# A hybrid decoder step on one core: the weight-quarter sums of every second channel tile of the up-projection, made early and kept in DRAM

## The chip, the core and the metric

The kernel runs on one core of a Trainium2 chip. The metric is device time in microseconds: the median of several runs of the whole program. The core's engines work side by side and wait for each other through semaphores: TensorE (PE in the rows) for matrix products, VectorE (DVE), ScalarE (ACT) and GpSimd (POOL) for elementwise work, and queues on SyncE (SP) and GpSimd that start transfers between DRAM and on-chip memory.

## The reference

One inference step of one decoder layer, for a prompt of 2064 tokens (16 of them learned) and 8 samples of one token. All is float32. Cut to the trunk and the part that the change touches:

```
def conv_ffn(h, hist, w_up, conv_w, conv_b, w_down):
    L = h.shape[1]
    up = h @ w_up                       # 1024 -> 2 x 2816
    g, v = up[..., :D_FF], up[..., D_FF:]
    ext = jnp.concatenate([hist.astype(g.dtype), g], axis=1)
    c = conv_b + conv_w[0] * ext[:, 0:L]
    for k in range(1, CONV_W):
        c = c + conv_w[k] * ext[:, k:k + L]
    out = (jax.nn.gelu(c) * v) @ w_down
    return out, ext[:, -(CONV_W - 1):]

def trunk(x, ...):
        h = rmsnorm(x, norm1_g[l])
        proj = h @ w_in[l]              # u_pool | u_ssm | gate_pool | gate_ssm
        y_pool, hp = pool_mixer(u_pool, ...)
        y_s, hr, hi = ssm_mixer(u_ssm, ...)
        y_ssm = glu_out(y_s, w_glu[l])
        x = x + (gate_pool * y_pool + gate_ssm * y_ssm) @ w_out[l]
        h2 = rmsnorm(x, norm2_g[l])
        f, hc = conv_ffn(h2, st_conv[l], w_up[l], conv_w[l], conv_b[l], w_down[l])
        x = x + f
        y = rmsnorm(x, norm_f_g)
```

## The kernel before

Every float32 product is made of three matmuls on values split into a rounded high and a low part (`split`: ACT casts the high part, L125; DVE or GpSimd subtracts it for the low part, L126; `mm3`: the matmuls of L144 to L146).

The program runs in stages. First the tokens are normalized piece by piece (`norm_piece`: DVE multiplies by the norm and the weight g1B at L258, PE transposes at L194), and the first part's input projections (sixteen calls of `u_ssm` and `u_pool`) and gates (`gate_ssm` eight times, `gate_pool` four times) are made, to about 224 us. Then come the setup of the state-space model (its tile mul is filled by GpSimd from L546 on), the model itself with the second part's gates (to about 690 us), the merge, the output projection and second norm (to about 1110 us), the up-projection with convolution (to about 2012 us), and the down-projection.

The up-projection is a 2x2 block product by seven products in place of eight (Winograd's form of Strassen's scheme). A call of `up(s, f, ...)` here is named a turn: s is one of three parts of the tokens, f one of 22 tiles of 128 channels, and a turn has 7 products of 12 matmuls of 128x344, 84 in all. The weights of a turn are four quarters of 128 partitions x 4 x 128: a11 and a12 of the gate columns' rows (wr1), a21 and a22 of the value columns' (wr2). The scheme needs four sums of them, s3 = a11 - a21, s1 = a21 + a22, s2 = s1 - a11 and s4 = a12 - s2. `w_ops(s, f)` makes them on GpSimd for s = 0 (L1129 to L1132), and SP stores them in DRAM (`WS`, 256 and 768 KB); for s = 1 and 2 it loads them from there instead of a21, with a11, a12 and a22. The weights are made two tiles ahead of their turn.

Products leave PSUM through ACT's copies (m and u, L1177) and DVE's additions into g (L1185, L1187). In part 0 ACT then copies the samples' columns (gsamp, L1195), GpSimd makes v (L1189) and moves two columns of g (L1196), and ACT and DVE make the convolution c (L1207 to L1216). The seventh product of a turn, and what follows it, is done by `up_end` inside the next turn: DVE multiplies one half of c by the product, GpSimd the other by v (L1224). For odd f, `up_end` (so in the turn of the next even f) also makes the combinations e that the down-projection needs, on DVE (L1244 to L1247), and GpSimd stores c and e in DRAM (`SD`, L1239).

The order on each engine is fixed when the program is built: a scheduler places instructions by priority and by their place in the code. Within an engine's row nothing overtakes.

Of the kernel before, what the change touches and what calls it, by code (L numbers as in the profile page):

```python
# [9 lines left out]
F32 = mybir.dt.float32  # L10
# [5 lines left out]
MUL, ADD, SUB, MAX = ALU.mult, ALU.add, ALU.subtract, ALU.max  # L16
# [3 lines left out]
P = 128  # L20
D = 1024
KT = 8
DFF = 2816
NF = 22
# [18 lines left out]
NU = 2 * NH * NSB  # L43
NT = 1024
WIN = (2, 4, 8, 16)


def _bits(x, n):
# [14 lines left out]
def hybrid_kernel(ctx, tc, x_prompt, x_sample, state_pool, state_re, state_im, state_conv, meta,  # L63
# [4 lines left out]
    V, S, T, GP = nc.vector, nc.scalar, nc.tensor, nc.gpsimd  # L68
    dma, gdma = nc.sync.dma_start, nc.gpsimd.dma_start
# [3 lines left out]
    w_in, w_glu, w_out, w_up, w_down = w_in[0], w_glu[0], w_out[0], w_up[0], w_down[0]  # L73
    pool_w = pool_w[0]

    def pool(name, bufs=1, space=None, side=None):
        kw = dict(name=name, bufs=bufs)
        if space is not None:
            kw["space"] = space
        if side is not None:  # L80
            kw["side"] = side
        if space is not DRAM:
            kw["reuse_waits"] = "tile"
        return tc.tile_pool(**kw)
# [7 lines left out]
    def bank(tag, name):  # L92
        return psum.tile([P, 512], F32, tag=tag, name=name, bufs=4)
# [12 lines left out]
    WS = dram.tile([NF, P, 4, 4, P], F32, name="WS")  # L106
# [96 lines left out]
    h1pool = gsc.enter_context(pool("h1pool"))  # L203
    evac = gsc.enter_context(pool("evac"))
    h0ctx = ExitStack()
    h0pool = h0ctx.enter_context(pool("h0pool"))
    hT = []
    for j, (a, b) in enumerate(PIECES):
# [11 lines left out]
    def norm_piece(j):  # L220
        a, b = PIECES[j]
        tiles = []
        off = 0
        if j == 0:
            tiles.append((0, 24, None))
            off = 24
        while off < b - a:
            tiles.append((off, P, a + off - 24))
            off += P
        ss = xpool.tile([P, 4], F32, tag="ss", name=f"ss_{j}", bufs=2)  # L230
        rs = xpool.tile([P, 4], F32, tag="rs", name=f"rs_{j}", bufs=2)
        if j == 0:
            V.memset(ss[:, 0:1], 1.0)
            tiles = [tiles[1], tiles[0], tiles[2]]
        xs = []
        for i, (o, m, p0) in enumerate(tiles):
            i = (1, 0, 2)[i] if j == 0 else i
            xt = xpool.tile([P, D], F32, tag="xt", name=f"xt_{j}_{i}", bufs=4)
            if p0 is None:
                dma(xt[0:14, :], meta[0:14, :])  # L240
                dma(xt[14:22, :], x_sample)
                dma(xt[22:24, :], meta[14:16, :])
            else:
                dma(xt, x_prompt[p0:p0 + P, :])
            xs.append((i, xt))
        for (o, m, p0), (i, xt) in zip(tiles, xs):
            junk = xpool.tile([P, D], BF16, tag="junk", name=f"junk_{j}_{i}", bufs=1)
            S.activation(junk[0:m], xt[0:m], AF.Square, accum_out=ss[0:m, i:i + 1])
            if j == 0:
                rsqrt(xpool, rs[:, i:i + 1], ss[:, i:i + 1], 1, f"n1_{j}_{i}")  # L250
        if j == 0:
            dma(g1B, norm1_g[0].partition_broadcast(P))
        else:
            rsqrt(xpool, rs[:, 0:len(tiles)], ss[:, 0:len(tiles)], len(tiles), f"n1_{j}")
        for (o, m, p0), (i, xt) in zip(tiles, xs):
            for q in range(2):
                c = slice(512 * q, 512 * (q + 1))
                V.scalar_tensor_tensor(xt[0:m, c], xt[0:m, c], rs[0:m, i:i + 1], g1B[0:m, c], op0=MUL, op1=MUL)  # L258
            transpose_split(xt, m, hT[j][0], hT[j][1], o, f"n1_{j}_{i}")
# [9 lines left out]
    def w_in_tile(m, name, eng=None):  # L269
        return load_w([(0, KT, w_in[:, m * P:(m + 1) * P].rearrange("(k p) c -> p k c", p=P))], name, eng)  # L270
# [25 lines left out]
    def u_pool(m, j, w):  # L296
# [17 lines left out]
        else:  # L314
            S.copy(up[:, 0:n], ps[:, 0:n])
            dma(rows[:, 16 + a - 8:16 + b - 8], up[:, 0:n])
            if j == 5:
# [3 lines left out]
                if m == 3:  # L321
                    dma(pool_p[0, 0], psamp[0:15, :])

    norm_piece(0)
    u_cols = (4, 5, 6, 7, 0, 1, 2, 3)
    u_w = [w_in_tile(m, f"u0_{m}", GP) for m in u_cols[:2]]
    norm_piece(1)
    for n, (i, j) in enumerate([(0, 0), (1, 0), (0, 1), (1, 1)] + [(i, j) for i in range(2, 8) for j in PARTS[0]]):
        m = u_cols[i]
        if i == len(u_w):  # L330
            u_w.append(w_in_tile(m, f"u0_{m}"))
        (u_ssm if m >= 4 else u_pool)(m % 4, j, u_w[i])
        if n in (1, 5, 9, 13):
            norm_piece(2 + n // 4)
    with tc.issue_after(w_ins[0]):

        vrow = xpool.tile([P, P], F32, tag="sr", name="vrow", bufs=2)
        for r0, n, ap in ((0, 8, norm1_g), (8, 8, norm2_g), (16, 8, pool_scale), (24, NF, conv_b), (46, 3 * NF, conv_w)):
            src = ap.rearrange("o (k p) -> (o k) p", p=P) if ap is not conv_w else ap[0].rearrange("w (k p) -> (w k) p", p=P)
            dma(vrow[r0:r0 + n, 0:P], src)  # L340
        pt = bank("B", "pt_c")
        T.transpose(pt[:, 0:112], vrow[0:112, 0:P], ident[0:112, 0:112])
        V.tensor_copy(colv, pt[:, 0:112])
        dma(pool_s[0, :, 0:14, :].rearrange("b r c -> b (r c)"),
            state_pool[:, 1:15, :].rearrange("b r c -> b (r c)"))
        dma(conv_s[0, :, 0, :], state_conv[:, 1, :])

        sv = state_conv.rearrange("b k (f p) -> (b k f) p", p=P)
        stv = stT.rearrange("p b k f -> p (b k f)")
        for r0 in range(0, 352, P):  # L350
            n = min(P, 352 - r0)
            sr = xpool.tile([P, P], F32, tag="sr", name=f"sr_{r0}", bufs=2)
            dma(sr[0:n], sv[r0:r0 + n])
            pq = bank("B", f"psc_{r0}")
            T.transpose(pq[:, 0:n], sr[0:n], ident[0:n, 0:n])
            V.tensor_copy(stv[:, r0:r0 + n], pq[:, 0:n])

        st = xpool.tile([120, 512], F32, name="st")
        dma(st, state_pool.rearrange("b r c -> (b r) c"))
        for g, w in enumerate(WIN):  # L360
            pq = bank("B", f"pst_{g}")
            T.transpose(pq[:, 0:120], st[:, g * P:(g + 1) * P], ident[0:120, 0:120])
            V.tensor_reduce(ssum[:, g, :], pq[:, 0:120].rearrange("p (b r) -> p b r", b=NS)[:, :, 16 - w:15],
                            axis=mybir.AxisListType.X, op=ADD)
# [7 lines left out]
    def pool_d(g, j):  # L372

        a, b = PIECES[j]
        w = WIN[g]
        pos0 = a - 8 if j else 14
# [66 lines left out]
    for m in range(8):  # L443
        for _ in gate_ssm(m, 0):
            pass
    for g in range(4):
        for _ in gate_pool(g, 0):
            pass
    h0ctx.close()


# [361 lines left out]
    for c in range(2):  # L813
        rows = slice(c * P, (c + 1) * P)
# [289 lines left out]
    def w_ops(s, f):  # L1104


        r1 = upA.tile([P, KT, P], F32, tag="r", name=f"wr1_{s}_{f}", bufs=4)
        r2 = upA.tile([P, KT, P], F32, tag="r", name=f"wr2_{s}_{f}", bufs=4)
        st = upA.tile([P, 3, 4, P], F32, tag="st", name=f"ws_{s}_{f}", bufs=2)
        later(r1, w_up[:, f * P:(f + 1) * P].rearrange("(k p) c -> p k c", p=P))  # L1110
        value = w_up[:, DFF + f * P:DFF + (f + 1) * P].rearrange("(k p) c -> p k c", p=P)
        ops = {}

        def sp(key, src):
            if (s, f) == (0, 0) and key in ORDER[:3]:
                hi, lo = [fw0.tile([P, 4, P], F32R, name=f"w{n}0_{key}") for n in "hl"]
            else:
                made[0] += 1
                pl, n = (fw, 6) if made[0] % 9 < 6 else (fw2, 3)
                hi = pl.tile([P, 4, P], F32R, tag="wh", name=f"wh{key}_{s}_{f}", bufs=n)  # L1120
                lo = pl.tile([P, 4, P], F32R, tag="wl", name=f"wl{key}_{s}_{f}", bufs=n)
            split(src, hi, lo)
            ops[key] = (hi, lo)

        a11, a12, a21, a22 = r1[:, 0:4, :], r1[:, 4:8, :], r2[:, 0:4, :], r2[:, 4:8, :]
        s1, (s2, s3, s4) = a21, [st[:, i] for i in range(3)]
        if s == 0:
            later(r2, value)
            GP.tensor_tensor(s3, a11, a21, op=SUB)  # L1129
            GP.tensor_tensor(s1, a21, a22, op=ADD)  # L1130
            GP.tensor_tensor(s2, s1, a11, op=SUB)
            GP.tensor_tensor(s4, a12, s2, op=SUB)  # L1132
            later(WS[f, :, 0], s1)
            later(WS[f, :, 1:4], st)
        else:
            later(s1, WS[f, :, 0])
            later(st, WS[f, :, 1:4])
            later(a22, value[:, 4:8])
        srcs = {1: a11, 6: s2, 7: s3, 5: s1, 3: s4, 4: a22, 2: a12}

        def make(key):
            if key not in ops:
                sp(key, srcs[key])
            return ops[key]

        return make
# [434 lines left out]
```

## Time and profile before

| | |
|---|---|
| runs | 2485.01, 2492.08, 2494.64 us; median 2492.08 us |
| profiled execution | 2488.14 us, span 2486.4 us from first to last instruction |
| mean granted clock of PE | 0.985 of full speed |
| busy over the span | PE 2387.1 us (96%), DVE 1688.9 (68%), ACT 980.3 (39%), GpSimd 942.2 (38%) |
| moved by DMA | 429.25 MB, 173 GB/s |

Busy time of PE is matmuls only; its weight loads run beside them. The granted clock is the speed that the chip's throttle allowed PE, relative to full speed. Idle time of an engine costs something only where another engine, in the end PE, waits for what it should have made. The rows shown below come from the page of the profiled execution and from views of its trace.

### The profile page before, as it was taken

What the parts mean: (1) busy time and instruction counts of PE and PEld (TensorE: products, weight loads), DVE (VectorE), ACT (ScalarE), POOL (GpSimd) and SP (SyncE); (2) the same over time, 40 slices, a digit from 0 to 9 for tenths busy, and PEclk for the clock granted to TensorE, in tenths of its full rate; (3) what the DMA queues carried; (4) which work ended last, traced back from release to release, by engine and by line L of the source; (5) the groups of instructions that cost most, each with busy time, mean ns of one, the idle gap of its engine ahead of it and who ended that gap; (6) DMA issues with size and microseconds to landing.
All of it is one profiled execution on the core that took longest, in us unless ns stands there. A gap on an engine that the chain in (4) does not pass through costs nothing. (4 is left out here: it accounts for less than half of the span.)

```text
span 2486.4 us, 37900 instructions
## 1 busy us (share of the span) xinstructions
PE 2387.1 (96%) x13628; PEld 2225.6 (90%) x13628; DVE 1688.9 (68%) x2916; ACT 980.3 (39%) x1814; POOL 942.2 (38%) x1189
## 2 busy tenths in 40 slices
PE   7999999999999999978899999999999999999997
PEld 6999999999999978878889999999999987878876
DVE  7635779987384244479888987678777764555766
ACT  5422222222342122254444555556555543332432
POOL 1000287985023220147666543233333223331383
PEclk9999999999999999999999999999999999999999
DMA  7544533333477666565555665555655578645673
GB/s 197 169 126 114 103 111 109 111 111 110 103 210 221 174 206 180 170 187 168 177 173 173 209 205 193 180 173 173 211 185 189 178 223 274 215 149 170 210 247 120
DMA packets 431375, 429.25 MB, mean 173 GB/s; under 512 B 89612, under 2 KB 353160, under 8 KB 431171
## 3 DMA queue, kind: packets, MB, share of 16 engines
q1 hardware_dynamic: 394723, 356.77, 47.9%
q0 software_dynamic: 11120, 40.40, 4.7%
q10 hardware_dynamic: 25344, 29.66, 3.4%
q8 instruction: 107, 1.75, 0.3%
q14 instruction: 81, 0.66, 0.1%
HBM read 297.20 MB, written 129.86 MB: 172 GB/s over the span
## 5 line engine op out<-in xcount | busy, mean ns | idle before, releaser
L144 PE MATMUL puX<-x,wh 128*128 128x344 f32 x1056 | 344.0, 329 | 31.3 <-ACT u L1177 16.7
L145 PE MATMUL puX<-x,wh 128*128 128x344 f32 x1056 | 344.4, 326 | 1.1 <-DVE x L126 1.1
L146 PE MATMUL puX<-x,wl 128*128 128x344 f32 x1056 | 340.3, 325 | 0.0
L1499 PE MATMUL pd<-th,sh 128*128 128x512 f32 x600 | 236.2, 396 | 3.6 <-ACT sh L125 2.7
L1501 PE MATMUL pd<-th,sl 128*128 128x512 f32 x600 | 236.5, 396 | 3.1 <-DVE sl L126 3.1
L1500 PE MATMUL pd<-tl,sh 128*128 128x512 f32 x600 | 238.3, 397 | 0.6 <-DVE tl L126 0.6
L126 DVE TENSOR_TENSOR wl<-wr,wh 128x512 fp32r<-128x512 f32 x264 | 214.0, 814 | 32.2 <-ACT wh L125 31.5
L144 PEld LDWEIGHTS puX<-x,wh 128*128 128x128 f32 x1056 | 202.9, 193 | 36.3 <-ACT u L1177 19.9
L125 ACT CAST wh<-wr 128x512 fp32r<-128x512 f32 x264 | 163.0, 619 | 162.3 <-PE puX L145 93.0
L126 DVE TENSOR_TENSOR sl<-sr,sh 128x512 fp32r<-128x512 f32 x154 | 134.7, 908 | 116.7 <-ACT sh L125 113.6
L145 PEld LDWEIGHTS puX<-x,wh 128*128 128x128 f32 x1056 | 203.5, 193 | 1.5 <-DVE x L126 1.4
L1274 POOL TENSOR_TENSOR tr<-tr,tr 128x512 f32<-128x512 f32 x77 | 111.1, 1444 | 244.2 <-DMA tr<-in_w_down_dram 235.7
L146 PEld LDWEIGHTS puX<-x,wl 128*128 128x128 f32 x1056 | 203.1, 193 | 0.0
L126 DVE TENSOR_TENSOR wl<-ws,wh 128x512 fp32r<-128x512 f32 x198 | 169.9, 864 | 43.7 <-ACT wh L125 43.5
L144 PE MATMUL puZ<-x,wh 128*128 128x344 f32 x528 | 169.9, 322 | 2.7 <-DVE g L1185 2.7
L146 PE MATMUL puZ<-x,wl 128*128 128x344 f32 x528 | 168.8, 320 | 2.0 <-DVE wl L126 2.0
L145 PE MATMUL puZ<-x,wh 128*128 128x344 f32 x528 | 169.5, 321 | 0.0
L125 ACT CAST wh<-ws 128x512 fp32r<-128x512 f32 x198 | 122.0, 619 | 103.3 <-PE puX L145 73.4
L125 ACT CAST sh<-sr 128x512 fp32r<-128x512 f32 x154 | 88.3, 618 | 177.5 <-PE pd L1500 154.5
L1499 PEld LDWEIGHTS pd<-th,sh 128*128 128x128 f32 x600 | 114.1, 190 | 31.9 <-ACT sh L125 3.2
L1501 PEld LDWEIGHTS pd<-th,sl 128*128 128x128 f32 x600 | 113.9, 190 | 29.3 <-DVE sl L126 4.2
L1500 PEld LDWEIGHTS pd<-tl,sh 128*128 128x128 f32 x600 | 114.1, 190 | 25.9 <-DVE tl L126 1.0
(532 smaller groups left out, 6696.2 us busy)
## 6 DMA issues: line engine op xcount, KB each, us to landing
wr<-in_w_up_dram SPq DMA_DIRECT2D x88, 512.0 KB
tr<-in_w_down_dram SPq DMA_DIRECT2D x150, 256.0 KB
sr<-SD SPq DMA_DIRECT2D x70, 512.0 KB
ws<-WS SPq DMA_DIRECT2D x44, 768.0 KB
WS<-ws SPq DMA_DIRECT2D x22, 768.0 KB
SD<-c POOLq DMA_DIRECT2D x44, 344.0 KB, 3.5
SD<-e POOLq DMA_DIRECT2D x22, 516.0 KB, 7.3
wr<-WS SPq DMA_DIRECT2D x44, 256.0 KB
```

The source lines that it names most:

```text
L125: S.copy(hi, raw)
L126: return (eng or V).tensor_tensor(lo, raw, hi.bitcast(F32), op=SUB)
L144: T.matmul(ps, wh, xh, start=start, stop=False, **kw)
L145: T.matmul(ps, wh, xl, start=False, stop=False, **kw)
L146: T.matmul(ps, wl, xh, start=False, stop=stop, **kw)
L1274: GP.tensor_tensor(raws[0], raws[0], raws[n + 1], op=op)
L1499: T.matmul(acc[j], xh[:, c], th, start=k == 0, stop=False)
L1500: T.matmul(acc[j], xh[:, c], tl, start=False, stop=False)
L1501: T.matmul(acc[j], xl[:, c], th, start=False, stop=k == NP - 1)
```

## The change

For even f, a generator `pre_sums` makes the four sums at the beginning of the program, in two units for each f (each with half of the rows): four loads of 128x2x128 from w_up and one store into WS, all from GpSimd's queue, and four GpSimd operations of 128x256 between them. A unit's tile is in a pool of two buffers. The code calls for a unit after each of the last ten of the sixteen projections, after each `gate_ssm` and after each `gate_pool`: 22 units. In `w_ops`, part 0 of an even f then loads as parts 1 and 2 do; part 0 of an odd f is as before. Lines of the up-projection stand 24 further down than before (L1129 is L1153, L1196 is L1220, L1224 is L1248).

```
+PRE = range(0, NF, 2)
...
     h0ctx = ExitStack()
+    pre = h0ctx.enter_context(pool("pre"))
...
+    def pre_sums():
+
+        for f in PRE:
+            for h in range(2):
+                t = pre.tile([P, 4, 2, P], F32, tag="pre", name=f"pre_{f}_{h}", bufs=2)
+                a22, a11, a21, a12 = [t[:, i] for i in range(4)]
+                for a, k, c in ((a22, 4, DFF), (a11, 0, 0), (a21, 0, DFF), (a12, 4, 0)):
+                    rows, cols = (k + 2 * h) * P, c + f * P
+                    gdma(a, w_up[rows:rows + 2 * P, cols:cols + P].rearrange("(k p) c -> p k c", p=P))
+                GP.tensor_tensor(a22, a21, a22, op=ADD)
+                GP.tensor_tensor(a21, a11, a21, op=SUB)
+                GP.tensor_tensor(a11, a22, a11, op=SUB)
+                GP.tensor_tensor(a12, a12, a11, op=SUB)
+                gdma(WS[f, :, :, 2 * h:2 * h + 2, :], t)
+                yield
+
+    pre_units = pre_sums()
...
         if n in (1, 5, 9, 13):
             norm_piece(2 + n // 4)
+        if n >= 6:
+            next(pre_units)
...
     for m in range(8):
         for _ in gate_ssm(m, 0):
             pass
+        next(pre_units)
     for g in range(4):
         for _ in gate_pool(g, 0):
             pass
+        next(pre_units)
     h0ctx.close()
...
-        if s == 0:
+        if s == 0 and f not in PRE:
             later(r2, value)
             GP.tensor_tensor(s3, a11, a21, op=SUB)
             GP.tensor_tensor(s1, a21, a22, op=ADD)
```

GpSimd's row in part 0, in the turn of f = 8, right after the columns of g of f = 7 are moved; ws and wr are the weight tiles of the turn two or three ahead. Before:

```order
L1196 COPY g_0_7_12863<-g_0_7_12863 128x2
L1189 TENSOR_TENSOR v_0_7_12864<-u3_0_7_12868,m5_0_7_12867 128x344
L1129 TENSOR_TENSOR ws_0_10_13293<-wr1_0_10_13291,wr2_0_10_13292 128x512
L1224 TENSOR_TENSOR c_0_7_12964<-c_0_7_12964,v_0_7_12864 128x344
L1130 TENSOR_TENSOR wr2_0_10_13292<-wr2_0_10_13292 128x512
L1226 COPY asamp_10214<-c_0_7_12964 128x8
L1131 TENSOR_TENSOR ws_0_10_13293<-wr2_0_10_13292,wr1_0_10_13291 128x512
L1239 DMA SD0_81<-c_0_6_12810 256x1x336
L1239 DMA SD1_82<-c_0_7_12964 256x1x336
L1132 TENSOR_TENSOR ws_0_10_13293<-wr1_0_10_13291,ws_0_10_13293 128x512
L1239 DMA SD2_83<-e_0_7_13064 384x1x336
```

The same place after the change:

```order
L1220 COPY g_0_7_13071<-g_0_7_13071 128x2
L1213 TENSOR_TENSOR v_0_7_13072<-u3_0_7_13076,m5_0_7_13075 128x344
L1248 TENSOR_TENSOR c_0_7_13172<-c_0_7_13172,v_0_7_13072 128x344
L1250 COPY asamp_10438<-c_0_7_13172 128x8
L1263 DMA SD0_81<-c_0_6_13018 256x1x336
L1263 DMA SD1_82<-c_0_7_13172 256x1x336
L1263 DMA SD2_83<-e_0_7_13268 384x1x336
L1214 COPY hist_10436<-g_0_8_13221 128x2
L1220 COPY g_0_8_13221<-g_0_8_13221 128x2
L1153 TENSOR_TENSOR ws_0_11_13655<-wr1_0_11_13653,wr2_0_11_13654 128x512
L1213 TENSOR_TENSOR v_0_8_13222<-u3_0_8_13226,m5_0_8_13225 128x344
```

The four sums of f = 10 that stood around c and the stores are gone from this row; the sums of f = 11, whose place was and is behind them, now begin between the moved columns of f = 8 and its v.

GpSimd's row at the start of the program, where ident is the matrix for PE's transposes, us are tiles of the state-space input, and wlo is the low part of the first two input weights. Before:

```order
masks.py:197 MEMSET ident_84 128x128
L281 MEMSET us_0_0_345 128x8x16
L281 MEMSET us_1_0_379 128x8x16
masks.py:199 ISA
masks.py:199 AFFINE_SELECT ident_84<-ident_84 128x128
L126 TENSOR_TENSOR wlo_u0_4_231<-raw_u0_4_229,whi_u0_4_230 128x1024
L126 TENSOR_TENSOR wlo_u0_5_237<-raw_u0_5_235,whi_u0_5_236 128x1024
```

After the change, the same place:

```order
L283 MEMSET us_1_0_382 128x8x16
L334 DMA pre_0_0_713<-in_w_up_dram 128x2x128
masks.py:199 ISA
masks.py:199 AFFINE_SELECT ident_84<-ident_84 128x128
L334 DMA pre_0_0_713<-in_w_up_dram 128x2x128 x3
L334 DMA pre_0_1_751<-in_w_up_dram 128x2x128 x4
L127 TENSOR_TENSOR wlo_u0_4_234<-raw_u0_4_232,whi_u0_4_233 128x1024
L335 TENSOR_TENSOR pre_0_0_713<-pre_0_0_713 128x256
L127 TENSOR_TENSOR wlo_u0_5_240<-raw_u0_5_238,whi_u0_5_239 128x1024
L336 TENSOR_TENSOR pre_0_0_713<-pre_0_0_713 128x256
L335 TENSOR_TENSOR pre_0_1_751<-pre_0_1_751 128x256
```

The loads of the first two units stand ahead of wlo, and their sums around the second wlo, in front of the seventh projection's place in the code.

## Rows read from the trace of the kernel before

**Rows 1.** The page's slices: PE's busy tenths, 40 slices of 62 us.

```profile
PE   7999999999999999978899999999999999999997
```

**Rows 2.** Windows: length, busy us (instructions) of PE, PEld, DVE, ACT, POOL; clock, DMA, GB/s.

```profile
0.00:25.00 25.00, 7.40 (x37) 6.38 (x38) 16.44 (x51) 13.74 (x23) 6.28 (x10) 1.00 0.75 226
25.00:125.00 100.00, 95.75 (x648) 93.55 (x648) 67.09 (x182) 48.61 (x87) 0.86 (x6) 0.98 0.61 172
125.00:240.00 115.00, 115.00 (x757) 114.34 (x756) 48.38 (x133) 29.52 (x54) 1.48 (x43) 1.00 0.42 120
...
1126.00:1481.00 355.00, 321.66 (x1929) 316.19 (x1929) 312.09 (x415) 172.97 (x328) 222.94 (x227) 0.96 0.58 184
1481.00:1707.00 226.00, 226.00 (x1431) 226.00 (x1430) 162.41 (x241) 124.80 (x222) 72.30 (x96) 1.00 0.57 185
```

**Rows 3.** Waits, 1126 to 1481 us: engine, line, waited for: us, times, longest.

```profile
ACT gsamp L1195 <- DVE g L1187: 76.4, 18, 7.8
...
ACT c L1207 <- POOL g L1196: 25.2, 11, 4.0
...
PE puX L144 <- ACT u L1177: 16.7, 8, 3.4
...
PE puX L144 <- ACT m L1177: 10.0, 4, 4.8
...
PE puX L144 <- ACT wh L125: 4.6, 2, 2.9
```

**Rows 4.** Timeline, one turn: start us, duration us, instruction [idle before, releaser].

```profile
1247.06 1.29 POOL L1129 TENSOR_TENSOR ws<-wr,wr 128x512 f32<-128x512 f32 x1 [1.71 <-DMA wr<-in_w_up_dram]
...
1248.30 0.93 POOL L1224 TENSOR_TENSOR c<-c,v 128x344 f32<-128x344 f32 x1
...
1249.27 1.58 DVE L1244 TENSOR_TENSOR e<-c,c 128x344 f32<-128x344 f32 x1 [2.66 <-POOL c L1224]
...
1258.28 0.21 ACT L1195 COPY gsamp<-g 128x8 f32<-128x8 f32 x1 [7.63 <-DVE g L1187]
```

**Rows 5.** Timeline of PE: two of its waits for u.

```profile
1150.27 0.62 PE L144 MATMUL puX<-x,wh 128*128 128x344 f32 x1 [3.43 <-ACT u L1177]
...
1259.39 0.53 PE L144 MATMUL puX<-x,wh 128*128 128x344 f32 x1 [3.23 <-ACT u L1177]
```

**Rows 6.** Tile wr, 1126 to 1481 us: ns min/median/max, first and last start.

```profile
L126 DVE TENSOR_TENSOR wl<-wr,wh x93: 672/684/2092, 1129.2 to 1480.9; 128x512 fp32r<-128x512 f32 x93
...
L1130 POOL TENSOR_TENSOR wr<-wr x18: 1280/1613/1741, 1126.8 to 1390.0; 128x512 f32<-128x512 f32 x18
...
L1129 POOL TENSOR_TENSOR ws<-wr,wr x17: 1283/1370/1850, 1136.7 to 1388.6; 128x512 f32<-128x512 f32 x17
```

**Rows 7.** Line L1239, GpSimd's stores: issue ns min/median/max, and their landing.

```profile
L1239 POOL DMA_DIRECT2D SD<-c x66: 672/682/788, 1136.0 to 2021.2; - x66
...
DMA to landing us min/median/max: 2.7/4.4/9.5
```

**Rows 8.** Line L732, a GpSimd sum of another stage: ns min/median/max.

```profile
L732 POOL TENSOR_TENSOR sinT<-TSt,TCt x32: 651/852/1634, 273.8 to 614.1; 128x272 f32<-128x272 f32 x32
```

**Rows 9.** Timeline of the start, DVE, GpSimd and PE.

```profile
9.97 1.42 DVE L258 SCALAR_TENSOR_TENSOR xt<-xt,rs,g1B 128x512 f32<-128x512 f32 x2 [0.87 <-DMA g1B<-in_norm_g_dram]
...
12.37 3.50 DVE L258 SCALAR_TENSOR_TENSOR xt<-xt,rs,g1B 24x512 f32<-24x512 f32 x2
...
12.79 5.30 POOL L126 TENSOR_TENSOR wlo_u<-raw_u,whi_u 128x1024 fp32r<-128x1024 f32 x2 [11.23 <-ACT whi_u L125]
...
81.27 0.33 PE L194 MATMUL ptr_n<-ident,xt 128*128 128x128 f32 x1 [3.80 <-DVE xt L258]
```

**Rows 10.** Tile mul: ns min/median/max, first and last start.

```profile
L546 POOL MEMSET mul<- x9: 98/98/99, 224.4 to 224.6; 128x1 f32 x9
L561 DVE TENSOR_TENSOR ta<-ph,mul x8: 226/327/433, 238.9 to 266.6; 128x72 f32<-128x72 f32 x4, 128x264 f32<-128x264 f32 x4
```

**Rows 11.** Timeline of GpSimd in the setup of the state-space model.

```profile
289.80 0.77 POOL L681 TENSOR_TENSOR f<-BA,X 128x128 f32<-128x128 f32 x2 [2.86 <-DMA BA<-in_ssm_B_re_dram]
```

## The prediction

> **What bounds the kernel now.** I read the slices of the span first. The PE digit is 9 nearly everywhere [rows 1], so a change is worth what it gives PE back in the few places where PE is short of work. The two lower places late in the row are the stage between the merge and the up-projection; the change leaves that stage as it is. The up-projection behind it shows 9, but a slice hides how far from full PE is.
>
> So next the busy time by stage [rows 2]. The first of the three token parts (1126 to 1481 us) has 1929 matmuls in 355 us. The second part, in 1481 to 1707, has 1431 in 226 us with PE busy all of it: 6.332 matmuls per us. At that rate the first part would need 1929 / 6.332 = 304.6 us, so it loses **50.4 us**. Two rows tell how. PE is busy 321.66 of 355 us, so 33.3 us are idle. The rest, 17.1 us, is clock: the granted clock is 0.96 there and 1.00 in the second part, a mean between the two levels, 2.4 GHz with some 8% of the time at 1.2. So one idle microsecond costs 50.4 / 33.3 = 1.51 us in this stage. Only this part makes sums of weight quarters: GpSimd is busy 222.94 us, and in the second part 72.30.
>
> Then the waits of the first part [rows 3]. PE's waits are for ACT: u (16.7 us, 8 times), m (10.0, 4 times), wh (4.6, twice); 2.0 us remain. ACT copies u and m out of PSUM, and they are late because ACT stands behind its gsamp copy, which waits for g of DVE (L1187) 76.4 us in all. The timeline of one turn shows why g is late [rows 4]: GpSimd's first sum L1129 waits 1.71 us for its weights. Behind it in GpSimd's queue stands L1224, the product c. DVE's e (L1244) waits 2.66 us for that c, so the whole e chain is late, the g addition behind it on DVE too, and gsamp waits 7.63 us. PE then waits 3.23 us for u [rows 5]. That is the turn which ends a pair of channel tiles: the turn of an even f, in which GpSimd makes the sums of the even tile two ahead. Of the ten waits for u and wh, nine (1167 to 1385 us) lie in such turns; one, 3.43 us at 1150.27, lies in an odd turn [rows 5]. The even turns' share is 16.7 + 4.6 - 3.4 = **17.9 us idle**.
>
> **The change, part by part.**
>
> *Sums of even f leave the first part.* GpSimd loses half of its four sums per tile (1.37 us for L1129 and 1.61 for L1130 by the medians [rows 6], about 6 us per tile), and above all those that stand in front of c in the turn with the long DVE chain. After it c follows v at once, and e starts when DVE reaches it. I take all of the even turns' waits off: 17.9 x 1.51 = **-27 us**. The odd turns hold 3.4 us for u and 10.0 - 4.8 = 5.2 for m (its longest, 4.8 us, is at the passage to the second part and stays). These have their own cause: the copy L1196 of g on GpSimd, for which ACT waits 25.2 us. They could go too (8.6 x 1.51 = 13 us) or grow; I take **-2**. The removed sums also hold DVE less: wl takes 0.672 us alone and up to 2.09 in the first part [rows 6]. What that is worth beyond this is the first rival.
>
> *Loads in place of stores.* An even tile in part 0 now loads what parts 1 and 2 load, 0.75 MB more, and stores 1 MB less. The DMA share there is 0.58 in the first part and 0.57 in the second [rows 2], where the same loads leave PE without an idle microsecond. Price 0, hidden by the first part's own matmuls; the weights are fetched two tiles ahead, 26 us.
>
> *The units.* Each of 22 units issues four loads of 128 KB and one store of 512 KB from GpSimd and makes four sums of 128x256. GpSimd has room: 6.28 us busy of the first 25, 0.86 of the next 100, 1.48 of the next 115 [rows 2]. An issue takes 0.68 us, a landing 4.4 (2.7 to 9.5) [rows 7]. A sum of 128x256 doesn't occur; between half of L1129's 1.37, 0.69, and the 0.85 of a 128x272 [rows 8] I take 0.75. Two units have two buffers, so they go in pairs: eight load issues 5.5, the last landing 4.4, then four sums (the other unit's lie beside its partner's loads) 3.0, two stores 1.4, their landing 4.4: 18.7 us. Eleven pairs are 206; with some 10 at the start, where GpSimd has two other operations of 5.3 us together, they end near **216 us** (174 with landings of 2.7 us at both places, 328 with 9.5).
>
> *Their price at the start.* The order has the first two units' loads and sums at the program's start, though the code issues them at the seventh projection. There three things lie on the path, since PE idles until the first normalized rows come. (a) 1 MB of loads enters ahead of or beside g1B, for which DVE waits at 9.97 us [rows 9]. At 226 GB/s and a share of 0.75 all engines give 301 GB/s: 1.05 MB take 3.5 us. Between 0 and 3.5 I take 3, since DMA is the busiest here of all stages. (b) Eight sums hold DVE. While GpSimd ran its 5.30 us from 12.79, DVE's two 24x512 took 3.50 us; the two 128x512 before, as long in each partition, took 1.42 [rows 9]. That is 2.1 us lost in 3.1 us of overlap, 0.67 per us. Eight sums are 6.0 us: 4.0 us, between 0 and 4.7; I take 4. (c) Later pieces: from 25 to 125 us the DMA share is 0.61 at 172 GB/s; ten units, about 10.5 MB, take 37 us at their quotient of 282 and bring it to 0.98, and 30 us of sums at 0.67 bring DVE from 67 to 87 us of 100. PE runs dry there when a piece is late, as now at 81.27 for 3.80 us [rows 9]. The memsets of the us and up tiles, too, now stand on GpSimd behind a unit's loads; each tile's copies out of PSUM wait for them. Between 0 and 6 I take 3. Together **+10** (0 to 14).
>
> *Their price at the end.* The memsets of mul stand on GpSimd behind 21 of the units. They run at 224.4 now and DVE needs them at 238.9 [rows 10]; setup on GpSimd has another 5 us (it waits 2.86 us for a DMA at 289.80 [rows 11]). Units done by 216 are free; from about 244 each microsecond moves the SSM stage. Price 0.
>
> **Sum.** 2488.1 + 10 - 27 - 2 = **2469 us**, against the profiled execution (2488.14), which stands 0.16% below the median of the runs (2492.08).
>
> **The rivals.**
>
> *A. DVE is set free as well, and all of the first part's loss goes.* DVE has 312.09 us for 1929 matmuls, 0.162 each, and 0.1135 in the second part: 93 us more, where 18 tiles' sums at 6 us take 108. If the loss is in proportion to the sums, half of it, 46 us, comes back: 266 us in 23 turns, 11.6 each, under the 13.27 of PE's turn at full rate (84 / 6.332). Then odd turns have no wait either: 2488 - 50 + 10 = **2448**. Against it: the light turns' waits hang on copies in a queue and not on DVE's sum.
> The Trainium skill (SBUF — State Buffer, section Who interferes with whom) says that a DVE instruction with two SBUF inputs and a GpSimd instruction that reads SBUF exclude each other, the later one blocked until the first is done. By that rule the result would be this rival's; the trace agrees in direction, since wl reaches 2.09 us against 0.672 [rows 6].
>
> *B. The wait moves to the odd tiles.* An odd tile's L1153 now stands before the next turn's v on GpSimd. It waits for its weights as L1129 does now (1.71 us [rows 4]). Eleven such waits, if each reaches PE, are 18.8 us idle, 28 us with the clock, and eat the whole gain: 2488 + 10 = 2498; with half of them 2488 + 10 - 29 + 14 = **2483**. For it: nothing in GpSimd's queue is early in this part, ACT's c alone waits 25.2 us for the copy L1196 [rows 3]. Against it: the odd turns have 8.6 us of waits now, with sums in GpSimd's queue too.
>
> *C. Slower: the units are not through in time.* A pair costs 9.9 us plus two landings. From (244 - 10) / 11 = 21.3 us per pair, landings of 5.7, the SSM stage slips up to one to one. At 263 us (landings of 6.6) the gain of 19 is gone; from 276 (7.1) the kernel is slower by over 0.5%. At landings of 7.5 the units end at 284: 2469 + 40 = **2509**. For it: landings go up to 9.5 [rows 7], and DMA is fuller here than in the stage of that row. Against it: the median is 4.4 at nearly the same share (0.58), and these loads are smaller.
> The Trainium skill (SBUF — State Buffer, section Who interferes with whom) puts a DMA that seems held by a DVE operation down to GpSimd's descriptor generation, starved of port time. That would lengthen these landings and make C likelier; no row here tells it from a full DMA.
>
> **How the numbers follow.** Forecast 0.54 with its own range 2458 to 2479 (start 0 to 14, odd turns 0 to -6 more); A 0.13, B 0.21, C 0.12. The range 2446 to 2490 leaves out C and the lower half of A, 0.18 in all. Half a per cent, 12.5 us, is about what this kernel's runs can tell from no change. Faster: A and 0.50 of the forecast, 0.63; within: B and the forecast's slow end, 0.25; slower: C, 0.12.
>
> **What would show it.** Right: the first part takes about 326 us with some 14 us of PE idle and a clock near 0.98; DVE's wait for c (L1248 after) is nearly gone; gsamp waits well under 76 us; the first matmuls run 6 to 8 us later; the mul memsets lie before 239. Wrong: waits for u or m in odd turns longer than 3.4 us behind L1153 (B), a first part near 305 us (A), mul memsets after 244 with PE idle before the SSM products (C), or a start that loses more than 14 us, for which nothing above has a price.

## The result, and the profile after

The changed kernel takes **2457.11 us** (median of 4 runs, 2456.17 to 2462.23) against 2491.01 before: a ratio of 0.9879, interval 0.9864 to 0.9893, or 30 us less. Run again beside later experiments, it was 0.9899 (0.9886 to 0.9913). The forecast was 19 us less, 2469, with 2446 to 2490 as its range. So the direction and the range held, but the time lies just below the forecast's own range, 2458 to 2479, on the way to rival A's 2448; the gain of the first part was larger, and so was the price of the start.

The profiled execution has a span of 2455.7 us, 30.7 less than before. Its windows, with the columns of [rows 2]; the fourth is the stretch between the same two matmuls of the first part (the 6350th and the 8250th of the program) as the row of before under it:

```profile
0.00:25.00 25.00, 6.82 (x31) 5.78 (x32) 13.65 (x43) 11.94 (x21) 16.60 (x25) 1.00 0.76 237
25.00:125.00 100.00, 89.17 (x575) 85.39 (x574) 68.01 (x170) 45.92 (x82) 64.15 (x88) 0.95 0.90 252
125.00:240.00 115.00, 114.13 (x756) 113.66 (x755) 54.73 (x83) 32.37 (x59) 77.35 (x121) 1.00 0.75 226
1132.60:1442.70 310.10, 303.71 (x1901) 301.88 (x1901) 274.65 (x410) 174.00 (x327) 174.62 (x192) 0.99 0.62 195
```

The kernel before, between those two matmuls:

```profile
1120.90:1471.60 350.70, 317.36 (x1903) 311.89 (x1902) 311.33 (x415) 170.81 (x325) 224.36 (x230) 0.96 0.58 184
```

At the second part's rate these 1900 matmuls would take 300.1 us. Before they lost 50.6 us, now 10.0: the first part gave 40.6. PE's idle time went from 33.3 to 6.4 us and the granted clock from 0.96 to 0.99. DVE is busy 36.7 us less, with 410 instructions against 415; that is the number that the forecast had set aside.

Most of it is three operations: the e of L1244, L1245 and L1247 (ns min/median/max; 12 of each). Before:

```profile
L1244 DVE TENSOR_TENSOR e<-c,c x12: 501/1582/1592, 1133.1 to 1462.6; 128x344 f32<-128x344 f32 x12
L1245 DVE TENSOR_TENSOR e<-e,c x12: 500/1596/1643, 1138.5 to 1463.4; 128x344 f32<-128x344 f32 x12
L1247 DVE TENSOR_TENSOR e<-c,e x12: 502/2442/2456, 1141.1 to 1465.9; 128x344 f32<-128x344 f32 x12
```

After:

```profile
L1268 DVE TENSOR_TENSOR e<-c,c x12: 502/504/1243, 1138.7 to 1435.3; 128x344 f32<-128x344 f32 x12
L1269 DVE TENSOR_TENSOR e<-e,c x12: 498/506/519, 1139.2 to 1435.9; 128x344 f32<-128x344 f32 x12
L1271 DVE TENSOR_TENSOR e<-c,e x12: 501/505/510, 1144.6 to 1438.4; 128x344 f32<-128x344 f32 x12
```

All 36 took 50.90 us before and 18.97 after, 31.9 of the 36.7 us. In the turn of [rows 4], before the change, each of the three ends 0.37 or 0.38 us after the GpSimd sum beside it:

```profile
1249.19 1.29 POOL L1130 TENSOR_TENSOR wr<-wr 128x512 f32<-128x512 f32 x1
1249.27 1.58 DVE L1244 TENSOR_TENSOR e<-c,c 128x344 f32<-128x344 f32 x1 [2.66 <-POOL c L1224]
...
1250.86 1.74 POOL L1131 TENSOR_TENSOR ws<-wr,wr 128x512 f32<-128x512 f32 x1
...
1251.38 1.60 DVE L1245 TENSOR_TENSOR e<-e,c 128x344 f32<-128x344 f32 x1
...
1254.35 2.44 DVE L1247 TENSOR_TENSOR e<-c,e 128x344 f32<-128x344 f32 x1
...
1254.90 1.51 POOL L1132 TENSOR_TENSOR ws<-wr,ws 128x512 f32<-128x512 f32 x1
```

The waits of the first part of the changed kernel (1117 to 1450 us), as in [rows 3]:

```profile
ACT c L1231 <- POOL g L1220: 34.0, 22, 5.4
...
ACT gsamp L1219 <- DVE g L1211: 23.8, 16, 5.7
...
POOL ws L1153 <- DMA wr<-in_w_up_dram: 19.6, 2, 12.0
...
PE puX L145 <- ACT u L1201: 4.3, 3, 1.7
...
PE puX L145 <- ACT m L1201: 1.8, 1, 1.8
DVE e L1268 <- POOL c L1248: 1.6, 2, 0.8
```

The last of these rows was, before:

```profile
DVE e L1244 <- POOL c L1224: 18.4, 8, 2.8
```

ACT's wait for g fell from 76.4 us to 23.8, PE's for u from 16.7 to 4.3 and for m from 10.0 to 1.8. ACT's wait for GpSimd's copy of g rose (25.2 to 34.0). Of the odd sums' two waits for weights the one of 12.0 us ends at 1116.3, ahead of the stretch, and the one of 7.6 us lies in it; PE's longest wait in the stretch is 1.8 us.

The start is where something was paid. The changed kernel's timeline there (start, duration, instruction, idle before it), for DVE, GpSimd, PE and ACT:

```profile
10.31 1.42 DVE L260 SCALAR_TENSOR_TENSOR xt<-xt,rs,g1B 128x512 f32<-128x512 f32 x2 [0.68 <-DMA g1B<-in_norm_g_dram]
...
14.13 1.04 ACT L126 CAST whi_u<-raw_u 128x1024 fp32r<-128x1024 f32 x1 [5.06 <-DMA raw_u<-in_w_in_dram]
...
15.26 2.35 POOL L127 TENSOR_TENSOR wlo_u<-raw_u,whi_u 128x1024 fp32r<-128x1024 f32 x1 [7.65 <-ACT whi_u L126]
...
18.36 3.93 DVE L260 SCALAR_TENSOR_TENSOR xt<-xt,rs,g1B 128x512 f32<-128x512 f32 x2
...
21.26 2.26 PE L195 MATMUL ptr_n<-ident,xt 128*128 128x128 f32 x8 [6.72 <-issue]
...
81.65 1.06 ACT L250 ACTIVATE junk<-xt 128x1024 bf16<-128x1024 f32 x1 [4.72 <-DMA xt<-in_x_prompt_dram]
...
94.53 1.76 PE L195 MATMUL ptr_n<-ident,xt 128*128 128x128 f32 x7 [6.70 <-DVE xt L260]
```

g1B lands at about the time that it did (DVE begins at 10.31 in place of 9.97 us). But the first weights come late: ACT's cast of raw_u, for whose load it waits, starts at 14.13 in place of 11.66, and GpSimd's wlo, 12.79 before, at 15.26. Before:

```profile
11.66 1.05 ACT L125 CAST whi_u<-raw_u 128x1024 fp32r<-128x1024 f32 x1 [2.82 <-DMA raw_u<-in_w_in_dram]
```

After the change a pair of L260 that runs into the second wlo and the sums takes 3.93 us, where an undisturbed pair takes 1.42; and PE's gap before 21.26, "issue" in both traces, is 6.72 us in place of 4.22. Later a piece of x comes late: ACT waits 4.72 us for it, and PE 6.70 at 94.53.

### The profile page after: what moved, and what is told of

It is laid out like the page before. It is cut to its first block, busy times and chain, and to the rows that moved or that the text cites. A ratio compares the mean times of both kernels' runs of the same rounds, so it can differ in the third digit from the quotient of the medians.

```text
span 2455.7 us, 38129 instructions
## 1 busy us (share of the span) xinstructions
PE 2376.1 (97%) x13628; PEld 2217.1 (90%) x13628; DVE 1660.0 (68%) x2916; ACT 983.2 (40%) x1814; POOL 1036.7 (42%) x1343
## 5 line engine op out<-in xcount | busy, mean ns | idle before, releaser
L145 PE MATMUL puX<-x,wh 128*128 128x344 f32 x1056 | 337.8, 323 | 6.1 <-ACT u L1201 4.3
L146 PE MATMUL puX<-x,wh 128*128 128x344 f32 x1056 | 339.5, 322 | 1.1 <-DVE x L127 1.1
L127 DVE TENSOR_TENSOR wl<-wr,wh 128x512 fp32r<-128x512 f32 x264 | 202.1, 770 | 31.2 <-ACT wh L126 30.8
L145 PEld LDWEIGHTS puX<-x,wh 128*128 128x128 f32 x1056 | 198.8, 189 | 7.4 <-ACT u L1201 5.2
L146 PEld LDWEIGHTS puX<-x,wh 128*128 128x128 f32 x1056 | 199.3, 189 | 1.5 <-DVE x L127 1.4
```

The lines of the kernel that those rows point to most:

```text
L127: return (eng or V).tensor_tensor(lo, raw, hi.bitcast(F32), op=SUB)
L145: T.matmul(ps, wh, xh, start=start, stop=False, **kw)
L146: T.matmul(ps, wh, xl, start=False, stop=False, **kw)
```

## The experiments

The kernel before ran beside every group of them (medians 2491 to 2494 us); the verdicts are the ratios. The stretch between the two matmuls of the first part is used for all. In the order of the matmuls (some stand in another order from build to build) the start can be read too:

```
start of matmul number     100     500    2000   (us)
before                    33.6    97.9   336.6
changed kernel            38.9   110.8   350.8
changed, run again        39.4   117.0   359.9
e1_odd                    40.2   116.4   359.9
e3_cost                   39.1   115.2   358.6
e4_nosum                  38.9   108.4   350.4
e2_free                   33.5   101.7   342.9
e5_pos                    34.2   100.8   340.8
e6_ms                     34.3   103.1   344.5
e9_late                   34.3   102.5   343.5
```

The profile of before lies at the low end of those that have no unit at the start (336.6 to 344.5), so a single trace shows the units' price too high or too low by several microseconds.

**Which tiles.** The odd tiles' sums are made early, the even ones stay where they were.

```
-PRE = range(0, NF, 2)
+PRE = range(1, NF, 2)
```

> The sums of the odd tiles, not of the even ones, are made early; everything else is as in the change. Theory P (place in the queue: the even tiles' sums stand in front of c in the turn with the e chain, so those sums are what must go): the even turns keep their 17.9 us of waits, 27 us with the clock; of the first part's loss of 50 only 23 goes, the start still costs 14: 2491 + 14 - 23 = 2482 us. Theory C (contention: GpSimd's sums, wherever they stand, hold DVE; half as many give DVE room enough): the same number of sums is gone, so the time is that of the change, 2457 us within 5, and DVE is busy 0.14 us per matmul in the first part.

Measured: 2474.17 us, ratio 0.9914 (0.9900 to 0.9929), and for the first part

```profile
1149.10:1460.80 311.70, 304.47 (x1901) 302.79 (x1901) 274.86 (x412) 172.49 (x326) 175.62 (x193) 0.99 0.62 198
```

311.7 us: the whole of the change's gain, with the sums of the even tiles still in front of c (DVE still waits 14.2 us for it, 8 times). Theory P asked for 328 or so. The e's still take 36.2 us here; other operations of DVE are shorter instead, and its busy time is that of the change. The total is 17 us above theory C's 2457. In the traces, 9 us of it are at the start (matmul 2000 at 359.9 us, as in the changed kernel when run again), and 7 between there and the first part (matmul 6350 at 1149.1 against 1132.6 us); what cost these 7 stays open. For the first part it doesn't matter which half of the tiles' sums goes.

**The gain without the units.**

```
-        if n >= 6:
-            next(pre_units)
...
-            later(s1, WS[f, :, 0])
-            later(st, WS[f, :, 1:4])
+            later(s1, WS[0 if f in PRE else f, :, 0])
+            later(st, WS[0 if f in PRE else f, :, 1:4])
```

> The early units are left out; from f = 2 on, the even tiles of all three parts load the stored sums of f = 0 (made inside the first part as before the change), so the outputs of those tiles are made with the sums of another tile, by the same transfers. This is the change without its price at the start. If the 14 us by which matmuls run late at 340 us are the units' price: 2457 - 14 = 2443 us, with the first matmuls where they were before and the first part as in the change. If they come from elsewhere (tiles placed otherwise, weights loaded otherwise): 2457 us.

Measured: 2451.53 us, ratio 0.9826 (0.9810 to 0.9842): 43 us less than before, the first part in 312.1 us. So the units cost some 13 us net, the difference of 0.9826 and 0.9879, or 18 by the change's second ratio, 0.9899.

**The units without the gain.**

```
-        if s == 0 and f not in PRE:
+        if s == 0:
...
-                gdma(WS[f, :, :, 2 * h:2 * h + 2, :], t)
+                gdma(WX[f, :, :, 2 * h:2 * h + 2, :], t)
```

> The units alone: they run as in the change but store into a tensor that nobody reads, and the first part makes all its sums as before. If the price of the units and the gain of the first part add up: 2491 + 14 = 2505 us. If waits between 700 and 1050 us take some of a late start back (3 us in the trace of the change): 2502. If the units aren't what costs: 2491.

Measured: 2510.38 us, ratio 1.0057 (1.0042 to 1.0072): 14 us more. The price and the gain add up: +14 and -43 make -29.

**What of the units costs.** The four GP.tensor_tensor lines of `pre_sums` are left out.

> The change with the four sums of each early unit left out (what is loaded is stored as it is, so the even tiles are made with other weights than they should be); loads and stores of the units stay. Without any unit the gain was 43 us, with them 30: the units cost 12.7 net. If their transfers cost it: 30 us faster than the kernel before, as the change, and PE's first 100 us as late as there. If their sums do, by holding DVE: 41 to 43 us faster. By the terms of the prediction (3 of 10 for the transfers, 4 to 7 for the sums) 36 to 39.

Measured: 2459.50 us, ratio 0.9864 (0.9849 to 0.9878): 34 us less than before. The interval touches that of the change, 0.9879 (0.9864 to 0.9893), and lies clear of 0.9826 without any unit. It also lies clear of the changed kernel when that ran again, on the same chip as this run: 0.9899 (0.9886 to 0.9913). Some 9 us of the price are therefore in the transfers; the sums' part is 4 us by the first ratio of the change, which isn't resolved, and 9 by the second, which is.

**The place in the queue.**

```
+            with tc.issue_after(c_of[f - 3]) if f % 2 == 0 and f - 3 in c_of else ExitStack():
                 GP.tensor_tensor(s3, a11, a21, op=SUB)
...
-        GP.tensor_tensor(c[:, NH:n], c[:, NH:n], v, op=MUL)
+        cg = GP.tensor_tensor(c[:, NH:n], c[:, NH:n], v, op=MUL)
         if s == 0:
+            c_of[f] = cg.ins
```

> The kernel before with one thing moved: in the first part the sums of an even f are queued on GpSimd behind c of tile f - 3, so c follows v at once. The number of sums, their operands and all transfers stay. Theory P: the even turns' waits go, 2491 - 27 = 2464 us, DVE's wait for c goes from 18.4 us to under 4. Theory C: DVE is held as long as before, 2491 us within 5, whatever the wait for c does.

Measured: 2482.65 us, ratio 0.9951 (0.9936 to 0.9966), 12 us less: between the two theories, nearer to C. In the first part

```profile
1125.40:1463.60 338.20, 313.24 (x1902) 305.85 (x1901) 319.19 (x411) 169.41 (x325) 227.28 (x230) 0.98 0.59 189
```

and of its waits (1125 to 1470 us)

```profile
ACT gsamp L1197 <- DVE g L1189: 69.6, 19, 7.3
...
PE puX L144 <- ACT u L1179: 15.4, 13, 3.6
...
PE puX L144 <- ACT m L1179: 7.8, 7, 3.0
...
DVE e L1247 <- POOL c L1226: 0.8, 1, 0.8
```

This is the row that decides against the forecast's mechanism as the main one. DVE's wait for c is gone, 18.4 to 0.8 us, as was meant, and PE still waits 15.4 us for u. DVE is busy 319.19 us, more than before, and its e's still take 47.66 us: c comes in time, and DVE is late all the same.

**The same time of GpSimd without reads.**

```
+            if f % 2 == 0:
+                for x in (s3, s1, s2, s4):
+                    for _ in range(3):
+                        GP.memset(x, 0.0)
+            else:
```

> The kernel before, no early units; in the first part each sum of an even f is replaced by three memsets of the same tile, so that GpSimd's queue keeps some of the time in the same place but nothing is read from on-chip memory there (the even tiles' sums are zeros, so their outputs aren't the reference's). Transfers stay as before. Theory P (place in the queue): c still waits behind them and behind the weights' DMA, the gain is at most the 12 us that moving the sums behind c gave. Theory C (two-input operations of DVE and GpSimd's reads hold each other): the first part falls to about 312 us as in the change, 35 to 40 us faster than before, and DVE's busy time there falls as in the change.

Measured: 2464.73 us, ratio 0.9883 (0.9867 to 0.9900), 29 us less. In the first part

```profile
1124.30:1450.50 326.20, 309.05 (x1902) 304.73 (x1901) 275.81 (x415) 174.73 (x329) 223.87 (x293) 0.98 0.63 197
```

and its memsets (min/median/max ns)

```profile
L1132 POOL MEMSET ws<- x72: 515/524/549, 1149.4 to 1353.9; 128x512 f32 x72
```

Three of 0.524 us take the place of one sum of 1.37 to 1.61 us, and GpSimd is as busy as before, 223.87 against 224.36 us. DVE's busy time falls by 35.5 us all the same, to what it is in the change (274.65), its e's take 19.18 us, and the first part is 24.5 us shorter. GpSimd's reads beside DVE's work are what costs DVE its time. The rest of the 40.6, 16 us, is likely GpSimd's queue; it is near to the 12.5 us that the moved sums gave in the run before. (A memset waits for one of the two weight loads at most, so some of the wait ahead of the sums is gone here too.)

**The units in another stage.** The units are put into the state-space stage, as quarter units, in place of the first 240 us.

```
-    pre = h0ctx.enter_context(pool("pre"))
+    prctx = ExitStack()
+    pre = prctx.enter_context(pool("pre"))
...
+            with tc.issue_after(gc_last[0]):
+                GP.tensor_tensor(a22, a21, a22, op=ADD)
...
             ssm_step(done)
             done += 1
+        if i >= 6 and i % 3 != 2:
+            next(pre_units, None)
```

> The change with the units elsewhere: in the state-space stage (300 to 690 us), as quarter units of 128x128, loaded and stored by SyncE's queue, the sums on GpSimd behind that stage's own additions; f = 0 is left to the first part. If a stage with PE digits of 9 and a DMA share near 0.4 takes them for nothing: the gain without the price, 40 to 43 us faster than before (2450). If GpSimd's additions there come late and PE with them, or DVE is held as in the first part: some of the 13 us is paid here instead, 2457 or later.

Measured: 2503.25 us, ratio 1.0036 (1.0023 to 1.0050), slower. The first part takes 310.2 us, as in the change; the loss is in the other stage. Windows of both stretches, and two waits of the first of them (330 to 720 us):

```profile
330.00:690.00 360.00, 327.58 (x1868) 301.29 (x1867) 283.91 (x545) 79.21 (x186) 302.38 (x586) 0.97 0.53 151
1170.20:1480.40 310.20, 303.67 (x1901) 301.86 (x1900) 274.18 (x411) 174.72 (x327) 175.32 (x192) 0.99 0.62 195
```

```profile
PE pyo L806 <- POOL gc L797: 27.4, 13, 5.0
...
POOL pre L351 <- DMA pre<-in_w_up_dram: 11.9, 6, 4.4
```

Before, in the same stage:

```profile
330.00:680.00 350.00, 349.93 (x2080) 329.97 (x2079) 271.49 (x579) 94.84 (x208) 232.43 (x417) 1.00 0.39 110
```

GpSimd, 232.43 of 350 us busy there before, is at 302.38 of 360 and waits for the units' loads besides; the model's own gc, which stands behind, comes late, and PE, idle for 0.07 us there before, waits 27.4 us for it. From matmul 2000 to 4000 the program takes 380.9 us, 336.5 before. A stage in which PE's digit is 9 isn't one that has room on GpSimd.

**The units later in the first stage.** Eight tiles, three buffers, and all loads behind the last memset of the up tiles. To make room, two small tiles of the setup have one buffer in place of two.

```
-PRE = range(0, NF, 2)
+PRE = range(6, NF, 2)
...
-            GP.memset(up[:, 0:16], 0.0)
+            ups[0] = GP.memset(up[:, 0:16], 0.0).ins
...
+            with tc.issue_after(ups[0]):
+                for i, (k, c) in enumerate(((4, DFF), (0, 0), (0, DFF), (4, 0))):
```

> The change with eight tiles (f = 6, 8, ... 20) in place of eleven, and with its units queued on GpSimd behind the last memset of the up tiles (some 92 us), three buffers in place of two; the other tiles as before the change. In the change the matmuls lost nothing more between 110 and 200 us while units ran on, so these 16 units should cost nothing there. If the gain of the first part (40 us for eleven tiles) goes with the number of sums that leave it: 29 us gained, 0 to 3 paid, 28 faster than before. If eight tiles are enough to free DVE, up to 38 faster. If the last units hold the setup of the state-space model: below 24.

Measured: 2459.01 us, ratio 0.9864 (0.9845 to 0.9883). The changed kernel ran beside it on the same chip:

> The changed kernel once more, beside the two others: 30 us faster than before (26 to 34).

It took 2468.28 us, ratio 0.9899 (0.9886 to 0.9913). So this version beats both kernels, the changed one by 9 us, with intervals that don't meet. The first of its loads starts at 89.2 us; its matmul 2000 starts at 343.5 us, as in kernels without units, and the first part takes

```profile
1129.10:1444.50 315.40, 306.82 (x1902) 305.65 (x1901) 274.54 (x412) 175.25 (x325) 188.43 (x198) 0.98 0.62 198
```

5.3 us more than with eleven tiles. Of the eleven even tiles only nine (f = 4 to 20) have their sums in this stretch; those of f = 0 and 2 are made ahead of it. So the fair proportion is eight of nine, 36.1 of 40.6 us, and the run keeps 35.3: the gain goes with the sums that leave the stretch.

**Fewer tiles, and the place for the others.** PRE = (4, 6, 10, 12, 16, 18), the units as in the last one, the other even tiles' sums behind c as in the run on the place.

> As the last, with six tiles (f = 4, 6, 10, 12, 16, 18), 12 units, and the sums of the even tiles that stay queued behind c of tile f - 3 (which alone, for all even tiles, gave 12 us). In proportion: 22 for the six tiles and 4 for the place of three others: 26 faster than before. If place and reading don't add up, 22.

Measured: 2464.07 us, ratio 0.9892 (0.9875 to 0.9909), 27 us less, with 317.1 us in the first part: 33.6 of the 40.6 us, where six of nine tiles would be 27.1; the rest is likely the moved sums'. It is not told apart from the changed kernel beside it.

## Why the prediction was right, and where it wasn't

**The loss of the first part** was read rightly: 50 us of idle time and clock, at 1.51 us for each idle microsecond. PE's idle time fell by 27.0 us, times 1.51 is 40.7, and 40.6 were measured. (Two readings on the way were off and changed nothing. Three slices are low in the middle of [rows 1], not two, and the two 8s lie in the first part itself; and one of the nine waits of even turns, 0.21 us, is at 1130.95, not from 1167 on.)

**The term -27 - 2 was mis-sized; it measured -40.6 us.** The step that failed is "I take all of the even turns' waits off", with the odd turns left as they were: the forecast took c's place behind the sums for the cause. That place is worth 12 us (the run that moves only it). The waits for m went too, from 10.0 to 1.8 us, with the one at the passage that was to stay. The larger part is what rival A said: DVE is short of time because GpSimd's sums hold it. Three runs show this from different sides. Taking off the odd tiles' sums, not in front of c, gives the same 39 us; leaving the place and taking off the reads gives 24.5; freeing the place and leaving the reads leaves DVE's busy time where it was. DVE's busy time per turn tells the same: 13.7 us before and 14.1 with only the place freed, both above the 13.27 of PE's turn at full rate, and 12.1 to 12.2 in the change and the two other runs.

Rival A's working was right to 5%, in part by luck: it put DVE at 266 us for 23 turns, 11.6 each; the row gives 274.65 for 1901 matmuls, 12.1 a turn. But its 93 us also count work that only the first part has, such as 81 operations on the samples' columns, 31.3 us, and DVE gave back 36.7 us where it had 46. Its result, all 50 us, was too much by the 10 that stay, of which 6.4 us are idle time of PE. DVE's additions with one operand in PSUM (L1185, L1187, L1223) take 0.50 to 0.51 us in both kernels; the e's, which got shorter, read both from SBUF, the on-chip memory that GpSimd's sums read too.
The Trainium skill (SBUF — State Buffer, section Who interferes with whom) has the rule that rival A named, and adds that a GpSimd instruction which only writes doesn't contend. The memsets' run agrees, 275.81 us of DVE against 311.33.

What should have tipped the balance stood in the trace of before: the e of [rows 4] takes 1.58 us, where 27 of them take 13.76 us in the second part, 0.51 each; and DVE's time per turn is longer than PE's. A waiting engine in a chain (c, then e, then g) was easier to see than the instructions of that chain that took three to five times as long.

That the time lies in the range is owed to the range, which takes in the upper half of rival A. The forecast's own sum had the gain of the first part 12 us too small and the price of the start 3 us or more too low, and the two errors partly cancel.

**Rival B did not come**: one odd sum in the stretch waited 7.6 us for its weights, and PE's longest wait is 1.8 us; whether its wait of 1.74 us for u at 1185.83, 10 us behind that sum, follows from it stays open. That the chain takes such a delay in because DVE has time is likely and not shown.

**The start, +10, was about right in sum and partly wrong in its terms.** By the ratios the units cost 13 us net, 18 when run again. (a) g1B came 0.34 us later, not 3; it was the first weights that came 2.5 us late, for which the forecast had no price. (b) isn't borne out. The pair of L260 took 2.5 us longer, but in the time of the second wlo (18.27 to 20.60) and of the sums behind it; without the sums the same pair starts at 20.97, PE's gap is 6.66 us, and matmul 100 starts at 38.9 all the same. So the 5 us of the first hundred matmuls (33 to 34 us without early units, 39 to 40 with them) belong to the units' transfers. (c) From matmul 100 to 500 kernels with the whole units take 71.9 to 77.6 us, with a piece of x late at DMA share 0.90, kernels without early units 64.3 to 68.8, and the one without the units' sums 69.5. Here the sums show. The forecast gave the transfers 3 us and the sums most of the rest; by the ratios the transfers hold 9, and the sums 4 to 9. What exactly delays the weights' and x's loads in a queue of their own wasn't tried.

**The pace of the units** was as worked out while they ran in pairs, and rival C not near:

```profile
L334 POOL DMA_DIRECT2D pre<-in_w_up_dram x88: 702/720/887, 1.4 to 218.9; - x88
...
DMA to landing us min/median/max: 2.5/5.0/8.1
```

Stores of successive pairs start at 154.3, 173.6 and 191.2 us, 19.3 and 17.6 apart for the 18.7 forecast. The last loads start at 218.9, and all but one of the last sums are through at 228.5, where the forecast had the end at 216 (its lower bound of 174 is 178 by its own terms). One sum and two stores stand behind the first mul memsets, which wait for PE and not for the units:

```profile
237.99 0.33 POOL L570 MEMSET mul<- 128x1 f32 x8 [9.46 <-PE pg L147]
```

DVE uses mul from 253.1 us, 238.9 before, as late as the matmuls are there.

**The loads in part 0** cost nothing that shows: PE's 6.4 us of idle time are, but for 0.2, behind ACT's u and m, none behind a transfer.

## What to carry to other kernels

When a stage loses time and several short waits point to one chain, compare first how long the same instruction takes in a stage without loss, and how busy each engine is per unit of work: instructions that take three to five times as long explain more than the wait that ended last. Elementwise work on VectorE and GpSimd side by side isn't free even with no dependency between them; moving half of GpSimd's sums out of this stretch gave 39.0 or 40.6 us, whichever half it was. Where they are moved to decides what is left of it (2503 us in the state-space stage, 2459 late in the first stage): DMA share and GpSimd's busy time of that stretch are to be read before PE's digits.

## What was not expected of the hardware

The same GpSimd time, 224 us, cost VectorE 36 us more as sums than half as sums and half as memsets. And the first 340 us of kernels that have the same work there differ by up to 8 us from one profiled execution to another (matmul 2000 at 336.6 to 344.5 us), while from matmul 8250 to 12000, through the second and third part, they all agree within 0.1 us. PE's longer waits in these starts are for normalized pieces of x; that their loads land at other times from run to run is likely, and wasn't tested.
